# First gate tile loaded early and in two parts, first products by token block, softmax division on ScalarE

## Chip, cores and metric

The kernel runs on one core of a Trainium2 chip. The metric is device time in microseconds of one execution, with the median over the runs shown. Five engines matter: TensorE (PE), VectorE (DVE), ScalarE (ACT), GpSimd (POOL) and SyncE (SP, which only issues DMAs here). Each works through its own instructions in order.

## What is computed

One layer of a decoder over 512 tokens of width 1024, cut here to what the text speaks of:

```
xn = rms_norm(h, norm1_g)
u, v, q, c_kv, q_idx, k_idx, w_idx, gates = split(xn @ w_in)
y_a = chunked_spatial_gating(u, v, ...)
qh  = partial_rope(rms_norm(q), positions)
att = softmax(qh . k over the 128 keys that the indexer picked, causal)
y_b = att @ vv
merged = sigmoid(g_A) * (y_a @ w_a_out) + sigmoid(g_B) * (y_b @ w_b_out)
h  = h + merged @ w_o
hn = rms_norm(h, norm2_g)
h  = h + peer(hn)
```

`peer` scores 128 x 128 experts by product keys, takes 16 of them for each of 8 heads and token, and sums gate * gelu(hn . u_e) * v_e over them.

## The kernel before

Tokens are four blocks of 128. Products that need float32 accuracy go through `mm3`: both operands are split into a high and a low part, and three products are summed. A weight tile (128 x 1024) comes through `load_w`: SP loads `wraw`, ACT casts it to `whi`, DVE makes `wlo` as the difference. So each weight passes SP's queue, ACT and DVE in turn.

*Start.* The four x tiles are loaded (L195), transposed on PE eight times each (L203) into `ps_tr`, and split into `xh` (ACT, L205) and `xl` (DVE, L207). In between, `ck_weights` loads four weight tiles; when all is there, `tok_group` makes the first products, one PSUM tile per token block.

*Mixers.* Column tiles (`pcol`) are products of xh, xl with the columns of w_in, for u and for the gates `sg`. Query tiles `qs` are normalized, rotated on DVE (`rope`, L338 to L343) and transposed on PE (`pq`, L442). The top 128 keys are found on DVE by repeated MAX and MATCH_REPLACE (L465, L466); the spatial gating adds and multiplies `zt` (L493, L494). `attend(b)` (L499 to L528) makes the logits of four heads (`pa`, PE), adds the mask and takes the maximum (DVE, L507), makes the Exp (ACT, L510), the reciprocal (DVE, L511) and the division (DVE, L512), transposes the weights `at` on PE (`ptr`, L518), copies them out of PSUM (`pT`, L520: DVE and ACT in turn), and multiplies by the values (`py`, L524).

*Experts.* For the first three token blocks (384 tokens) all experts are computed densely, as 128 groups of 128: `expert_in(j)` loads up-row tile Uj, makes `pa` (24 products, 384 columns) and its Gelu; groups 28 to 99 keep the result `actd` in DRAM (`ad`). Meanwhile the gates are written to DRAM as `gd`, in 24 chunks of 16 tokens (L840, on ACT's queue). The fourth block's experts are gathered row by row by POOL and handled on DVE.

*Final stage* (L844 to L903). For each of 128 groups j: load down-row tile Vj; `pr` = act * gate on DVE (L886); split into `ph` (ACT, L890) and `pl` (DVE, L891); 18 products into six PSUM tiles `y`. The gates come as tiles `gg`, one for eight groups, from all 24 chunks of gd (L872). The remaining 28 up-row tiles are handled in this stage as well.

The order of instructions on each engine is not the program's: a scheduler rearranges them by its own simulation (`schedule_with_timeline_sim`), within the dependences and the buffers of the pools. So an edit at one place can move instructions elsewhere.

Of the kernel before, what the change touches and what calls it, by code (L numbers as in the profile page):

```python
# [9 lines left out]
F32 = mybir.dt.float32  # L10
# [4 lines left out]
AF = mybir.ActivationFunctionType  # L15
# [5 lines left out]
P = 128  # L21
S = 512
# [38 lines left out]
def kernel(ctx: ExitStack, tc: tile.TileContext, x, pos, cst, wtok, wsm, wcol, wkv, spt,  # L61
# [81 lines left out]
    with ExitStack() as c1:  # L143
# [10 lines left out]
        def tok_group(src, lhs_h, lhs_l, name, keep=None, done=None, finish=None):  # L154

            ps = [mm.tile([P, S], F32, name=f"{name}{b}", tag="mm") for b in range(NB)]

            def part(kp, b, hi, lo):
                bs = slice(b * P, (b + 1) * P)
                for kk in range(2):  # L160
                    k = 2 * kp + kk
                    ks = slice(kk * 512, (kk + 1) * 512)
                    mm3(ps[b], lhs_h[:, k, bs], lhs_l[:, k, bs], hi[:, ks], lo[:, ks], k == 0, k == KC - 1)

            if keep is None:
                for kp in range(4):
                    hi, lo = load_w(src(kp))
                    for b in range(NB):
                        part(kp, b, hi, lo)
            else:  # L170
                ws = keep if src is None else [load_w(src(kp), keep, 2) for kp in range(4)]
                for b in range(NB):
                    for kp in range(4):
                        part(kp, b, *ws[kp])
                    if done and 0 < b < NB - 1:
                        done(b - 1, ps[b - 1])
                if done:
                    finish(ps)
            return ps
# [3 lines left out]
        with tc.tile_pool(name="xin", bufs=4, reuse_waits="tile") as xp:  # L183
# [2 lines left out]
            ssx = tp.tile([P, NB], F32, name="ssx")  # L186
            ws = []

            def ck_weights(kp):
                ws.append(load_w(wtok[8 + kp], xp, 2))  # L190

            xts = []
            for b in range(NB):
                xt = xp.tile([P, D], F32, name="xt")
                SY.dma_start(xt, x[b * P:(b + 1) * P, :])  # L195
                xts.append(xt)
                if b == 0:
                    SY.dma_start(g1c, g1b)
                bs = slice(b * P, (b + 1) * P)
                for k0 in range(0, KC, 4):  # L200
                    ps = mm.tile([P, 4, P], F32, name="ps_tr", tag="mm")
                    for k in range(4):
                        T.transpose(ps[:, k, :], xt[:, (k0 + k) * P:(k0 + k + 1) * P], ident)  # L203
                    for k in range(k0, k0 + 4):
                        sq_after = A.activation(xh[:, k, bs], ps[:, k - k0, :], AF.Copy, scale=g1c[:, k:k + 1])  # L205
                    for k in range(k0, k0 + 4):
                        V.scalar_tensor_tensor(xl[:, k, bs], ps[:, k - k0, :], g1c[:, k:k + 1],  # L207
                                               xh[:, k, bs].bitcast(F32), ALU.mult, ALU.subtract)
                for _ in range((1, 0, 1, 2)[b]):
                    ck_weights(len(ws))  # L210
            ps_ck = tok_group(None, xh, xl, "pt2", ws)
            junk = xp.tile([P, D], F32, name="junk", bufs=1)
            with tc.issue_after(sq_after.ins):
                for b in range(NB):
# [284 lines left out]
        def attend(b):  # L499
            n = (b + 1) * P  # L500
            ph = []
            for h in range(NH):
# [9 lines left out]
                V.tensor_scalar(t, t, mx[:, 3:4], None, ALU.mult)  # L512
                ph.append(t)
            pts = []
            for k in range(b + 1):
                pt = sm.tile([P, S], F32, name="ptr", tag="sm")
                for h in range(NH):
                    T.transpose(pt[:, h * P:(h + 1) * P], ph[h][:, k * P:(k + 1) * P], ident)  # L518
                pT = sc.tile([P, S], F32, name="pT", tag="w", bufs=NW)
                (A.copy if k % 2 else V.tensor_copy)(pT, pt)  # L520
# [322 lines left out]

    with ExitStack() as c3:  # L844
        yp = c3.enter_context(tc.tile_pool(name="yp", bufs=1, space=PSUM))
        wv = c3.enter_context(tc.tile_pool(name="wv", bufs=2, reuse_waits="tile"))
        gr = c3.enter_context(tc.tile_pool(name="gr", bufs=2, reuse_waits="tile"))
# [16 lines left out]
        def load_v(n):  # L864
            while len(vq) < min(n, P):
                vq.append(load_w(vt[len(vq)], wv, 4))

        load_v(2)
        for j in range(P):
            if j % JG == 0:  # L870
                gt = gr.tile([P, NCH, JG, TC], F32, name="gg", tag="gg")
                SY.dma_start(gt, gd[:, :, j:j + JG, :])  # L872
                if j + JG == P:
                    hr = gr.tile([P, NB - 1, D], F32, name="hr", tag="gg")
# [99 lines left out]
```

## Time and profile before

| | |
|---|---|
| runs | 1598.69 us median of 3 (1598.64 to 1601.45) |
| profiled execution | 1599.28 us, span 1597.2 us |
| PE busy | 1558.5 us (98%) |
| DVE busy | 1271.2 us (80%) |
| ACT busy | 646.3 us (40%) |
| POOL busy | 346.0 us (22%) |
| mean DMA rate | 247 GB/s |

The span is from the first to the last instruction; the execution's time has some 2 us around it. PE is busy nearly throughout, so what matters is where it is not. The mean DMA rate hides a low first third and a final stage between 284 and 370 GB/s in most of its slices. Busy shares are means over stages, and a stage is read through its own windows and waits. Releasers in the list of waits are inferred; a busy PE can run at half its clock, which the column PEclk shows.

### The profile page before, as it was taken

The numbers are of one execution on the slowest core, as the hardware profiler recorded it, in microseconds if no ns is written. First come the engines' busy times: TensorE is split into PE (matmuls) and PEld (weight loads), VectorE is DVE, ScalarE is ACT, GpSimd is POOL, SyncE is SP. The second block draws the span as 40 slices with busy tenths as digits, with TensorE's granted clock in tenths as the row PEclk, the third lists the DMA queues.
The fourth block names the chain that finished last, engine by engine and source line by source line (L and its number), as shares of the span: only waits on it lengthen the run. The fifth ranks groups of instructions, "written<-read, shape, count | busy, mean of one in ns | idle before, by whom it ended". The sixth has DMA issues, their size and how long they took to land.

```text
span 1597.2 us, 22620 instructions
## 1 busy us (share of the span) xinstructions
PE 1558.5 (98%) x8173; PEld 1355.2 (85%) x8173; DVE 1271.2 (80%) x2670; ACT 646.3 (40%) x954; POOL 346.0 (22%) x280
## 2 busy tenths in 40 slices
PE   8999999999999999999999989999999999999998
PEld 6777867888899999999999978888888888888777
DVE  6489974557999989999999657787877877888854
ACT  5453333323334335555666533333333333333232
POOL 0010000000000353323222213433322332334400
PEclk9999999999999999999999989999999999999999
DMA  6111224222223689999999999999999999998862
GB/s 218 66 66 67 93 75 176 93 93 93 89 83 120 225 299 342 345 339 341 368 338 344 355 315 312 314 351 344 370 335 342 338 334 328 342 328 306 284 226 95
DMA packets 160400, 395.01 MB, mean 247 GB/s; under 512 B 12960, under 2 KB 80544, under 8 KB 156704
## 3 DMA queue, kind: packets, MB, share of 16 engines
q1 hardware_dynamic: 109600, 220.01, 39.5%
q0 software_dynamic: 36864, 134.23, 23.7%
q10 hardware_dynamic: 13824, 39.33, 6.3%
q8 instruction: 64, 1.05, 0.3%
q14 instruction: 48, 0.39, 0.1%
HBM read 350.53 MB, written 42.99 MB: 246 GB/s over the span
## 4 chain that ended last, share of the span: by engine, by line
PE 75%; DMA 12%; issue 5%; DVE 5%; POOL 2%; ACT 0%; SPq 0%; POOLq 0%; DVEq 0%; ACTq 0%
PE pa L93 8%; PE pa L91 8%; PE pa L92 8%; PE y L92 7%; PE y L93 7%; PE y L91 7%; DMA gt<-in_v_rows,eid 5%; DMA gt<-in_u_rows,eid 3%; PE pg L836 2%; PE pcol L91 2%; PE pcol L92 2%; PE pcol L93 2%; POOL gt L658 2%; PE pq L91 2%; PE pq L92 2%
## 5 line engine op out<-in xcount | busy, mean ns | idle before, releaser
L86 ACT CAST whi<-wraw 128x1024 fp32r<-128x1024 f32 x320 | 335.0, 1053 | 332.2 <-PE pa L92 124.2
L87 DVE TENSOR_TENSOR wlo<-wraw,whi 128x1024 fp32r<-128x1024 f32 x320 | 389.3, 1219 | 79.9 <-ACT whi L86 69.9
L91 PE MATMUL pa<-hh,whi 128*128 128x384 f32 (+2 forms) x1040 | 349.8, 336 | 2.9 <-ACT actd L649 2.2
L93 PE MATMUL pa<-hh,wlo 128*128 128x384 f32 (+2 forms) x1040 | 348.6, 336 | 2.7 <-DVE wlo L87 2.7
L92 PE MATMUL pa<-hl,whi 128*128 128x384 f32 (+2 forms) x1040 | 348.4, 335 | 0.0
L92 PE MATMUL y<-wlo,ph 128*128 128x512 f32 x768 | 302.5, 394 | 4.7 <-DVE wlo L87 4.7
L93 PE MATMUL y<-whi,pl 128*128 128x512 f32 x768 | 299.0, 392 | 0.0
L658 POOL DMA_INDIRECT gt<-in_u_rows,eid x128 | 168.9, 1319 | 535.7 <-DVE dots L664 306.8
L658 POOL DMA_INDIRECT gt<-in_v_rows,eid x128 | 164.7, 1287 | 293.2 <-DVE h2l L673 263.4
L890 ACT CAST ph<-pr 128x384 fp32r<-128x384 f32 x128 | 65.8, 515 | 384.4 <-PE y L92 360.4
L91 PE MATMUL y<-whi,ph 128*128 128x512 f32 x768 | 209.3, 393 | 7.7 <-ACT ph L890 7.7
L93 PEld LDWEIGHTS pa<-hh,wlo 128*128 128x128 f32 x1040 | 195.4, 188 | 8.2 <-DVE wlo L87 4.2
L91 PEld LDWEIGHTS pa<-hh,whi 128*128 128x128 f32 x1040 | 195.5, 188 | 7.9 <-ACT actd L649 2.9
L92 PEld LDWEIGHTS pa<-hl,whi 128*128 128x128 f32 x1040 | 195.5, 188 | 4.1
L673 DVE SCALAR_TENSOR_TENSOR h2l<-gt,coef,h2l 128x1024 f32<-128x1024 f32 x128 | 163.8, 1280 | 25.7 <-DMA gt<-in_v_rows,eid 25.3
L92 PEld LDWEIGHTS y<-wlo,ph 128*128 128x128 f32 x768 | 145.0, 189 | 35.6 <-DVE wlo L87 6.4
L91 PEld LDWEIGHTS y<-whi,ph 128*128 128x128 f32 x768 | 144.3, 189 | 34.8 <-ACT ph L890 8.0
L664 DVE CUSTOM_DVE_ANT_0 gt<-gt,hn 128x1024 f32<-128x1024 f32 x128 | 155.6, 1218 | 17.8 <-DMA gt<-in_u_rows,eid 17.7
L93 PEld LDWEIGHTS y<-whi,pl 128*128 128x128 f32 x768 | 144.6, 188 | 28.2
L891 DVE TENSOR_TENSOR pl<-pr,ph 128x384 fp32r<-128x384 f32 x128 | 71.1, 556 | 89.9 <-ACT ph L890 82.4
L838 ACT ACTIVATE ch<-pg 128x512 f32<-128x512 f32 x96 | 96.7, 1113 | 30.0 <-PE pg L836 29.6
L886 DVE TENSOR_TENSOR pr<-act,gg 128x384 f32<-128x384 f32 x128 | 70.5, 554 | 11.2 <-DMA act<-ad 4.9
(305 smaller groups left out, 1925.3 us busy)
## 6 DMA issues: line engine op xcount, KB each, us to landing
wraw<-in_ut SPq DMA_DIRECT2D x128, 512.0 KB, 5.9
wraw<-in_v_rows SPq DMA_DIRECT2D x128, 512.0 KB, 6.3
gd<-ch ACTq DMA_DIRECT2D x24, 1024.0 KB, 6.6
gg<-gd SPq DMA_DIRECT2D x16, 1536.0 KB, 14.4
ad<-actd ACTq DMA_DIRECT2D x72, 192.0 KB, 5.5
act<-ad SPq DMA_DIRECT2D x72, 192.0 KB, 6.8
wraw<-in_wcol SPq DMA_DIRECT2D x20, 512.0 KB, 3.2
wraw<-in_wq SPq DMA_DIRECT2D x16, 512.0 KB, 3.2
```

Of the source, the lines that this page charges most:

```text
L86: A.copy(hi, raw)
L87: V.tensor_tensor(lo, raw, hi.bitcast(F32), ALU.subtract)
L91: T.matmul(ps, lh, rh, start=start, stop=False)
L92: T.matmul(ps, lh, rl, start=False, stop=False)
L93: return T.matmul(ps, ll, rh, start=False, stop=stop)
L658: G.indirect_dma_start(out=t, out_offset=None, in_=table, in_offset=bass.IndirectOffsetOnAxis(ap=eid[:, s:s + 1], axis=0))
L664: V.tensor_tensor_reduce(out=t, in0=t, in1=hn3, scale=1.0, scalar=0.0, op0=ALU.mult, op1=ALU.add, accum_out=dots[:, s:s + 1])
L673: V.scalar_tensor_tensor(h2l, t, coef[:, s:s + 1], h2l, ALU.mult, ALU.add)
L838: A.activation(ch[:, :, to + t4:to + t4 + 4].rearrange("p i t -> p t i"), pg, AF.Copy, scale=1.0 / GS)
L886: V.tensor_tensor(pr.rearrange("p (c t) -> p c t", c=NCH), acts[j].rearrange("p (c t) -> p c t", c=NCH), gt[:, :, j % JG, :], ALU.mult)
L890: A.copy(ph, pr)
L891: V.tensor_tensor(pl, pr, ph.bitcast(F32), ALU.subtract)
```

## The change

Three edits:

- At the start, one weight tile is loaded behind each x tile, the first products are written by token block and weight (`PARTS`) between the transposes, and `ps_tr` takes its buffers from the pool of three instead of the pool of five.
- In `attend`, the division is an ACT instruction (Copy with a scale per row) and all pT copies are on ACT.
- In the final stage, the pool of `gg` is split into two of one buffer; the first is taken ahead of the pool of the V weights. `load_g(0)` is written ahead of the V loads and loads chunks 0 to 22 and chunk 23 by a DMA each; other groups are loaded as before.

```
@@ -168,7 +168,7 @@
                     for b in range(NB):
                         part(kp, b, hi, lo)
             else:
-                ws = keep if src is None else [load_w(src(kp), keep, 2) for kp in range(4)]
+                ws = [load_w(src(kp), keep, 2) for kp in range(4)]
                 for b in range(NB):
                     for kp in range(4):
                         part(kp, b, *ws[kp])
@@ -186,9 +186,19 @@
             ssx = tp.tile([P, NB], F32, name="ssx")
             ws = []
 
-            def ck_weights(kp):
-                ws.append(load_w(wtok[8 + kp], xp, 2))
-
+
+            ps_ck = [mm.tile([P, S], F32, name=f"pt2{b}", tag="mm") for b in range(NB)]
+
+            def ck_part(kp, b):
+                hi, lo = ws[kp]
+                bs = slice(b * P, (b + 1) * P)
+                for kk in range(2):
+                    k = 2 * kp + kk
+                    ks = slice(kk * 512, (kk + 1) * 512)
+                    mm3(ps_ck[b], xh[:, k, bs], xl[:, k, bs], hi[:, ks], lo[:, ks], k == 0, k == KC - 1)
+
+            PARTS = ((), ((0, 0), (0, 1)), ((1, 0), (1, 1), (0, 2), (1, 2)),
+                     ((2, 0), (2, 1), (2, 2), (0, 3), (1, 3), (2, 3), (3, 0), (3, 1), (3, 2), (3, 3)))
             xts = []
             for b in range(NB):
                 xt = xp.tile([P, D], F32, name="xt")
@@ -198,7 +208,7 @@
                     SY.dma_start(g1c, g1b)
                 bs = slice(b * P, (b + 1) * P)
                 for k0 in range(0, KC, 4):
-                    ps = mm.tile([P, 4, P], F32, name="ps_tr", tag="mm")
+                    ps = sm.tile([P, 4, P], F32, name="ps_tr", tag="sm")
                     for k in range(4):
                         T.transpose(ps[:, k, :], xt[:, (k0 + k) * P:(k0 + k + 1) * P], ident)
                     for k in range(k0, k0 + 4):
@@ -206,9 +216,9 @@
                     for k in range(k0, k0 + 4):
                         V.scalar_tensor_tensor(xl[:, k, bs], ps[:, k - k0, :], g1c[:, k:k + 1],
                                                xh[:, k, bs].bitcast(F32), ALU.mult, ALU.subtract)
-                for _ in range((1, 0, 1, 2)[b]):
-                    ck_weights(len(ws))
-            ps_ck = tok_group(None, xh, xl, "pt2", ws)
+                ws.append(load_w(wtok[8 + b], xp, 2))
+                for kp, bb in PARTS[b]:
+                    ck_part(kp, bb)
             junk = xp.tile([P, D], F32, name="junk", bufs=1)
             with tc.issue_after(sq_after.ins):
                 for b in range(NB):
@@ -509,7 +519,7 @@
                 V.tensor_scalar(mx[:, 1:2], mx[:, 0:1], -ATT_SCALE, None, ALU.mult)
                 A.activation(t, t, AF.Exp, bias=mx[:, 1:2], scale=ATT_SCALE, accum_out=mx[:, 2:3])
                 V.reciprocal(mx[:, 3:4], mx[:, 2:3])
-                V.tensor_scalar(t, t, mx[:, 3:4], None, ALU.mult)
+                A.activation(t, t, AF.Copy, scale=mx[:, 3:4])
                 ph.append(t)
             pts = []
             for k in range(b + 1):
@@ -517,7 +527,7 @@
                 for h in range(NH):
                     T.transpose(pt[:, h * P:(h + 1) * P], ph[h][:, k * P:(k + 1) * P], ident)
                 pT = sc.tile([P, S], F32, name="pT", tag="w", bufs=NW)
-                (A.copy if k % 2 else V.tensor_copy)(pT, pt)
+                A.copy(pT, pt)
                 pts.append(pT)
             py = sm.tile([P, S], F32, name="py", tag="sm")
             for k in range(b + 1):
@@ -843,8 +853,9 @@
 
     with ExitStack() as c3:
         yp = c3.enter_context(tc.tile_pool(name="yp", bufs=1, space=PSUM))
+        gr = [c3.enter_context(tc.tile_pool(name="gr0", bufs=1, reuse_waits="tile"))]
         wv = c3.enter_context(tc.tile_pool(name="wv", bufs=2, reuse_waits="tile"))
-        gr = c3.enter_context(tc.tile_pool(name="gr", bufs=2, reuse_waits="tile"))
+        gr.append(c3.enter_context(tc.tile_pool(name="gr1", bufs=1, reuse_waits="tile")))
         cp = c3.enter_context(tc.tile_pool(name="cp", bufs=3, reuse_waits="tile"))
         ys = [[yp.tile([P, 512], F32, name=f"y{b}_{hf}") for hf in range(2)] for b in range(NB - 1)]
         vt = v_rows.rearrange("(i j) d -> i j d", j=P)
@@ -865,13 +876,20 @@
             while len(vq) < min(n, P):
                 vq.append(load_w(vt[len(vq)], wv, 4))
 
+        def load_g(i):
+
+            t = gr[i % 2].tile([P, NCH, JG, TC], F32, name="gg", tag="gg")
+            for c0, c1 in ((0, NCH - 1), (NCH - 1, NCH)) if i == 0 else ((0, NCH),):
+                SY.dma_start(t[:, c0:c1], gd[:, c0:c1, i * JG:(i + 1) * JG, :])
+            return t
+
+        gt0 = load_g(0)
         load_v(2)
         for j in range(P):
             if j % JG == 0:
-                gt = gr.tile([P, NCH, JG, TC], F32, name="gg", tag="gg")
-                SY.dma_start(gt, gd[:, :, j:j + JG, :])
+                gt = load_g(j // JG) if j else gt0
                 if j + JG == P:
-                    hr = gr.tile([P, NB - 1, D], F32, name="hr", tag="gg")
+                    hr = gr[P // JG % 2].tile([P, NB - 1, D], F32, name="hr", tag="gg")
                     SY.dma_start(hr, hd)
             room = max(KEPT - 5 - max(0, KEPT - j), 0) + max(0, j - AHEAD)
             while len(acts) < min(P, AHEAD + min(room, (P - AHEAD) * (j + 1) // (P - 4))):
```

The scheduler gives another order with it. Three places:

SP, the end of the up-row loads and the start of the down-row loads (in_ut are up-rows, in_v_rows down-rows; x98 stands for U2 to U99). Before, then with the change:

```order
43 L85 DMA wraw<-in_ut 128x1024 x98
44 L85 DMA wraw<-in_v_rows 128x1024 x2
45 L872 DMA gg<-gd 128x24x128
46 L85 DMA wraw<-in_v_rows 128x1024 x2
47 L872 DMA gg<-gd 128x24x128
48 L85 DMA wraw<-in_ut 128x1024 x2
```

```order
43 L85 DMA wraw<-in_ut 128x1024 x95
44 L883 DMA gg<-gd 128x23x128
45 L85 DMA wraw<-in_ut 128x1024 x3
46 L883 DMA gg<-gd 128x128
47 L85 DMA wraw<-in_v_rows 128x1024 x4
48 L883 DMA gg<-gd 128x24x128
49 L85 DMA wraw<-in_ut 128x1024 x2
```

The first gg is now two loads, one issued three up-row loads earlier and one directly ahead of V0; the second gg follows V3 as before.

PE, the fourth query block's attention: pa are logits, ptr the transposes of the softmax rows, pcol a column tile. Before, then with the change; shown are the rows at which the kind of work changes, and the row numbers tell what lies between.

```order
821 L504 MATMUL pa<-kT,qs_951 128x512 x2
822 L92 MATMUL pcol_2237<-xl,whi 128x512
829 L93 MATMUL pcol_2237<-xh,wlo 128x512
830 L504 MATMUL pa<-kT,qs_951 128x512 x2
831 L518 MATMUL ptr<-ident,at 128x128 x16
832 L524 MATMUL py<-pT,vv 128x512 x4
```

```order
818 L514 MATMUL pa<-kT,qs_951 128x512
819 L93 MATMUL pcol_2237<-xh,wlo 128x512
823 L91 MATMUL pcol_2237<-xh,whi 128x512
824 L528 MATMUL ptr<-ident,at 128x128
825 L92 MATMUL pcol_2237<-xl,whi 128x512
831 L528 MATMUL ptr<-ident,at 128x128
832 L92 MATMUL pcol_2237<-xl,whi 128x512
835 L92 MATMUL pcol_2237<-xl,whi 128x512
836 L528 MATMUL ptr<-ident,at 128x128 x2
837 L93 MATMUL pcol_2237<-xh,wlo 128x512
840 L93 MATMUL pcol_2237<-xh,wlo 128x512
841 L528 MATMUL ptr<-ident,at 128x128 x12
```

Before, all 16 transposes follow the last logits at once; now pcol products stand between them, 19 from the last logits to the last twelve transposes.

DVE, the end of the query rotation (qs_948 to qs_951 are the four blocks; sg a gate product). Before, then with the change, the rows of the halves that write qs and what stands between:

```order
269 L466 MATCH_REPLACE madd_646<-m_1303,madd_646 128x384
270 L342 TENSOR_TENSOR qs_948<-rp_990,rp_991 128x4x16
271 L343 TENSOR_TENSOR qs_948<-rp_992,rp_993 128x4x16
272 L342 TENSOR_TENSOR qs_949<-rp_1010,rp_1011 128x4x16
273 L343 TENSOR_TENSOR qs_949<-rp_1012,rp_1013 128x4x16
274 L536 TENSOR_TENSOR sg_1854<-pcol_1829,rxb 128x512
284 L87 TENSOR_TENSOR wlo<-wraw,whi 128x1024
286 L342 TENSOR_TENSOR qs_950<-rp_1030,rp_1031 128x4x16
287 L343 TENSOR_TENSOR qs_950<-rp_1032,rp_1033 128x4x16
289 L343 TENSOR_TENSOR qs_951<-rp_1052,rp_1053 128x4x16
```

```order
275 L476 MATCH_REPLACE madd_646<-m_1303,madd_646 128x384
276 L546 TENSOR_TENSOR sg_1854<-pcol_1829,rxb 128x512
277 L352 TENSOR_TENSOR qs_948<-rp_990,rp_991 128x4x16
278 L353 TENSOR_TENSOR qs_948<-rp_992,rp_993 128x4x16
279 L87 TENSOR_TENSOR wlo<-wraw,whi 128x1024
280 L352 TENSOR_TENSOR qs_949<-rp_1010,rp_1011 128x4x16
281 L353 TENSOR_TENSOR qs_949<-rp_1012,rp_1013 128x4x16
291 L476 MATCH_REPLACE madd_646<-m_1306,madd_646 128x384
292 L352 TENSOR_TENSOR qs_950<-rp_1030,rp_1031 128x4x16
293 L353 TENSOR_TENSOR qs_950<-rp_1032,rp_1033 128x4x16
295 L353 TENSOR_TENSOR qs_951<-rp_1052,rp_1053 128x4x16
```

The gate product now stands ahead of the first block's rotation and a wlo between the first and the second; the wlo ahead of the third is gone from there.

## Rows read from the trace of the kernel before

**Rows 1.** The page's part 1, whole span: busy us of each engine (share) xinstructions

```profile
PE 1558.5 (98%) x8173; PEld 1355.2 (85%) x8173; DVE 1271.2 (80%) x2670; ACT 646.3 (40%) x954; POOL 346.0 (22%) x280
```

**Rows 2.** Waits of PE, whole span: us in total, times, longest us

```profile
PE y L91 <- ACT ph L890: 7.7, 1, 7.7
...
PE ps_tr L203 <- DMA xt<-in_x: 7.7, 3, 4.2
...
PE y L92 <- DVE wlo L87: 4.7, 4, 1.5
...
PE pq L442 <- DVE qs L343: 3.3, 1, 3.3
...
PE ptr L518 <- DVE at L512: 2.5, 2, 2.4
```

**Rows 3.** PE's timeline at four places: start us, us, ..., [idle before <-releaser]

```profile
230.54 0.39 PE L91 MATMUL pcol<-xh,whi 128*128 128x512 f32 x1
230.77 0.39 PE L92 MATMUL pcol<-xl,whi 128*128 128x512 f32 x1
...
237.80 0.44 PE L518 MATMUL ptr<-ident,at 128*128 128x128 f32 x2 [2.38 <-DVE at L512]
...
909.59 0.44 PE L91 MATMUL pa<-hh,whi 128*128 128x384 f32 x1 [1.35 <-ACT actd L649]
...
925.90 0.79 PE L91 MATMUL y<-whi,ph 128*128 128x512 f32 x1 [7.72 <-ACT ph L890]
```

**Rows 4.** 3-us windows, 909 to 933: width, busy us (instructions), PEclk, DMA share, GB/s

```profile
909.00:912.00 3.00, 2.41 (x14) 2.41 (x15) 2.82 (x4) 1.03 (x3) 0.18 (x1) 1.00 0.84 253
...
924.00:927.00 3.00, 1.10 (x3) 0.91 (x4) 2.15 (x5) 0.98 (x2) 0.00 (x0) 0.50 1.07 358
927.00:930.00 3.00, 3.00 (x9) 2.32 (x8) 1.96 (x4) 0.51 (x1) 0.00 (x0) 0.50 1.21 291
930.00:933.00 3.00, 3.00 (x11) 2.39 (x10) 0.00 (x0) 0.51 (x1) 0.00 (x0) 0.70 1.11 358
```

**Rows 5.** SP's timeline, 897 to 909: start us of each load's issue

```profile
897.96 0.33 SPq L85 DMA_DIRECT2D wraw<-in_ut  x1
...
906.70 1.56 SPq L85 DMA_DIRECT2D wraw<-in_v_rows  x2
908.35 0.61 SPq L872 DMA_DIRECT2D gg<-gd  x1
```

**Rows 6.** ACT's timeline, 890 to 930: its last gd store and U97's cast

```profile
893.76 0.33 ACTq L840 DMA_DIRECT2D gd<-ch  x1
...
908.10 1.04 ACT L86 CAST whi<-wraw 128x1024 fp32r<-128x1024 f32 x1 [3.11 <-PE pa L92]
```

**Rows 7.** DMA of 890 to 930: a queue's packets, MB, share; issues with median us to landing

```profile
q1 hardware_dynamic: 6860, 7.56, 61.0%
...
wraw<-in_ut SPq DMA_DIRECT2D x6, 512.0 KB, 6.2
...
wraw<-in_v_rows SPq DMA_DIRECT2D x6, 512.0 KB, 7.4
...
gd<-ch ACTq DMA_DIRECT2D x1, 1024.0 KB, 8.4
```

**Rows 8.** A 4-us window in the fourth query block, columns as in rows 4

```profile
240.00:244.00 4.00, 4.00 (x11) 2.01 (x10) 0.16 (x1) 0.59 (x1) 0.00 (x0) 0.71 0.99 383
```

**Rows 9.** The page's part 6, whole span: KB each, us to landing

```profile
wraw<-in_v_rows SPq DMA_DIRECT2D x128, 512.0 KB, 6.3
```

**Rows 10.** Groups by line, whole span: xcount | busy us, mean ns | idle before

```profile
L510 ACT ACTIVATE at<-at,mx 128x128 f32<-128x128 f32 (+3 forms) x16 | 8.9, 556 | 14.4 <-DVE mx L509 14.3
...
L512 DVE TENSOR_SCALAR at<-at,mx 128x128 f32<-128x128 f32 (+3 forms) x16 | 5.9, 377 | 0.1
```

**Rows 11.** DVE's timeline in the fourth query block

```profile
234.83 1.22 DVE L87 TENSOR_TENSOR wlo<-wraw,whi 128x1024 fp32r<-128x1024 f32 x1
```

**Rows 12.** A 50-us window of the final stage, columns as in rows 4

```profile
1075.00:1125.00 50.00, 49.21 (x233) 42.40 (x232) 40.17 (x46) 17.61 (x24) 20.53 (x15) 1.00 0.99 353
```

More of the change, by code (lines that the diff above doesn't have):

```diff
@@ L170, in tok_group @@
             else:
-                ws = keep if src is None else [load_w(src(kp), keep, 2) for kp in range(4)]
+                ws = [load_w(src(kp), keep, 2) for kp in range(4)]
                 for b in range(NB):
@@ L187, with ck_part @@
             ws = []
-            def ck_weights(kp):
-                ws.append(load_w(wtok[8 + kp], xp, 2))
+            ps_ck = [mm.tile([P, S], F32, name=f"pt2{b}", tag="mm") for b in range(NB)]
+            def ck_part(kp, b):
+                hi, lo = ws[kp]
+                bs = slice(b * P, (b + 1) * P)
+                for kk in range(2):
+                    k = 2 * kp + kk
+                    ks = slice(kk * 512, (kk + 1) * 512)
+                    mm3(ps_ck[b], xh[:, k, bs], xl[:, k, bs], hi[:, ks], lo[:, ks], k == 0, k == KC - 1)
+            PARTS = ((), ((0, 0), (0, 1)), ((1, 0), (1, 1), (0, 2), (1, 2)),
+                     ((2, 0), (2, 1), (2, 2), (0, 3), (1, 3), (2, 3), (3, 0), (3, 1), (3, 2), (3, 3)))
             xts = []
@@ L200 @@
                 for k0 in range(0, KC, 4):
-                    ps = mm.tile([P, 4, P], F32, name="ps_tr", tag="mm")
+                    ps = sm.tile([P, 4, P], F32, name="ps_tr", tag="sm")
                     for k in range(4):
@@ L208 @@
                                                xh[:, k, bs].bitcast(F32), ALU.mult, ALU.subtract)
-                for _ in range((1, 0, 1, 2)[b]):
-                    ck_weights(len(ws))
-            ps_ck = tok_group(None, xh, xl, "pt2", ws)
+                ws.append(load_w(wtok[8 + b], xp, 2))
+                for kp, bb in PARTS[b]:
+                    ck_part(kp, bb)
             junk = xp.tile([P, D], F32, name="junk", bufs=1)
@@ L511, in attend @@
                 V.reciprocal(mx[:, 3:4], mx[:, 2:3])
-                V.tensor_scalar(t, t, mx[:, 3:4], None, ALU.mult)
+                A.activation(t, t, AF.Copy, scale=mx[:, 3:4])
                 ph.append(t)
@@ L519, in attend @@
                 pT = sc.tile([P, S], F32, name="pT", tag="w", bufs=NW)
-                (A.copy if k % 2 else V.tensor_copy)(pT, pt)
+                A.copy(pT, pt)
                 pts.append(pT)
@@ L845 @@
         yp = c3.enter_context(tc.tile_pool(name="yp", bufs=1, space=PSUM))
+        gr = [c3.enter_context(tc.tile_pool(name="gr0", bufs=1, reuse_waits="tile"))]
         wv = c3.enter_context(tc.tile_pool(name="wv", bufs=2, reuse_waits="tile"))
-        gr = c3.enter_context(tc.tile_pool(name="gr", bufs=2, reuse_waits="tile"))
+        gr.append(c3.enter_context(tc.tile_pool(name="gr1", bufs=1, reuse_waits="tile")))
         cp = c3.enter_context(tc.tile_pool(name="cp", bufs=3, reuse_waits="tile"))
@@ L866, in load_v, with load_g @@
                 vq.append(load_w(vt[len(vq)], wv, 4))
+        def load_g(i):
+            t = gr[i % 2].tile([P, NCH, JG, TC], F32, name="gg", tag="gg")
+            for c0, c1 in ((0, NCH - 1), (NCH - 1, NCH)) if i == 0 else ((0, NCH),):
+                SY.dma_start(t[:, c0:c1], gd[:, c0:c1, i * JG:(i + 1) * JG, :])
+            return t
+        gt0 = load_g(0)
         load_v(2)
@@ L870 @@
             if j % JG == 0:
-                gt = gr.tile([P, NCH, JG, TC], F32, name="gg", tag="gg")
-                SY.dma_start(gt, gd[:, :, j:j + JG, :])
+                gt = load_g(j // JG) if j else gt0
                 if j + JG == P:
-                    hr = gr.tile([P, NB - 1, D], F32, name="hr", tag="gg")
+                    hr = gr[P // JG % 2].tile([P, NB - 1, D], F32, name="hr", tag="gg")
                     SY.dma_start(hr, hd)
```

## The prediction

> **What bounds the kernel now.** I read the busy shares first, then what TensorE (PE) waits for, then the rows around its longest wait. PE is busy for 1558.5 of 1597.2 us [rows 1], so 38.7 us are all the idle time there is. The list of its waits names most of it [rows 2]: 7.7 us before the first product into y in the final stage, 7.7 us for x tiles at the start, 4.7 us for wlo in the final stage, 3.3 us for the rotated queries qs, 2.5 us for softmax rows `at`. The reader should see that only a few waits are there to be removed, and that a wait can cost more than itself: PE ends its last product before y at 918.18 and starts again at 925.90 [rows 3]; afterwards the granted clock stands at 0.50 (1.2 of 2.4 GHz) and comes back within 930 to 933 [rows 4].
>
> **Part 1, the first group's gates.** What PE waits for at 918.18 is ph, which ACT makes from pr, which multiplies by the tile gg. The load of gg was issued at 908.35 [rows 5], behind those of V0 and V1 (both from 906.70). Its source was complete before that: the last store of gd was issued at 893.76 [rows 6], and such a store takes 8.4 us [rows 7], so 902.2. The load was late because it stood late in SyncE's (SP's) order.
>
> The change issues 23 of its 24 chunks behind the weight load of U96, three loads before the old place of V0 (first piece of order above), and the last chunk, which alone needs the last store, behind U99. Both parts land well before PE needs them. What goes is 7.72 us of idle and the time lost at half clock behind it, which is PE's busy time multiplied by the missing clock in three windows [rows 4]: 1.10 x 0.50 + 3.00 x 0.50 + 3.00 x 0.30 = 2.95 us. Ceiling: 10.7 us.
>
> What takes its place: the DMA engines are full there (share 1.07 to 1.21 [rows 4]), so 1.5 MB put ahead of other loads delays them. Behind part 1 in SP's queue stand U97, U98, U99, the last chunk, V0 and V1. How long part 1 (23/24 of 1.57 MB, 1.51 MB) holds them up is bounded by two rates: all that the engines move, 336 GB/s (the mean of 358, 291 and 358 [rows 4]), gives 4.5 us; what SP's queue had of it, 7.56 MB in 40 us [rows 7], 189 GB/s, gives 8.0 us.
> - U97 was issued at 897.96 [rows 5] and such a load lands 6.2 us later [rows 7], near 904.2. Its cast on ACT began at 908.10, when PE let go of a buffer [rows 6]: slack 3.9 us. Late by 4.5 to 8.0, the cast starts 0.6 to 4.1 us later. ACT works in order; behind the cast stands the Gelu `actd` that frees a PSUM buffer of PE. PE already waits 1.35 us for it [rows 3], and that wait grows by 0.6 to 4.1 us.
> - V0 was issued at 906.70, so it was there after 7.4 us [rows 7], at 914.1; now at 918.6 to 922.1. With its cast (1.04 us, as in [rows 6]) y can start at 919.6 to 923.2. PE itself gets there at 918.8 to 922.3, so V0 is late next, by some 0.8 us.
>
> So y starts 2.7 to 6.3 us before 925.90, and with 2.95 us of clock part 1 brings 5.7 to 9.2. I take -7.5, the middle: the two rates are equally near.
>
> One rule bears on the grown wait. The rows show that the clock stayed at 1.00 around the wait of 1.35 us [rows 3, 4] and stood at a mean of 0.71 behind the wait of 2.38 us at 237.80 [rows 3, 8]. The Trainium skill, "TensorE: Matmul & The Clock Gate", Part 1, says that the throttled clock is the default and that activity releases it. By that rule a wait at 909 that has grown to 2.0 to 5.5 us may halve the clock too, and the gain would then be smaller by about the 1.2 us that the slow stretch at 240 cost (worked out below). I don't put it into the sum, since the products that it would slow have some 0.8 us until V0 comes; it widens the range.
>
> Against this part speaks a second rule. On full engines [rows 4] a load of a down-row took 7.4 us to land [rows 7], where the median of all 128 is 6.3 [rows 9]. The Trainium skill, "DMA: Bandwidth & Descriptors", in Queues, rings and completion order, says that each engine consumes the descriptors of one row in ring order. By it a load put in front pays for itself with the loads behind; that is the rival of the moved wait, below.
>
> **Part 2, the softmax.** 16 divisions leave VectorE (DVE), 5.9 us in all, 0.377 each [rows 10]. On ACT each costs about what the Exp of the same tiles does, 0.556 us [rows 10], together 8.9 us, on an engine that is busy 40% of the span [rows 1]. Neither sum is the term; PE's wait is. In the fourth query block a wlo of 1.22 us at 234.83 [rows 11] stands on DVE between the maxima and the last two Exps, PE has only transposes left in its order, and waits 2.38 us for the divisions [rows 3]. The change moves PE's order as well (second piece of order): between the last logits and the last twelve transposes now stand 19 column products that take 0.23 us each [rows 3], 4.4 us of cover. The wait of 2.5 us should go, and with it the slow stretch, 4.00 x 0.29 = 1.16 us in 240 to 244 [rows 8]: ceiling 3.7. I take -3.2, for the last two Exps and divisions still follow each other on ACT.
>
> The order changes at 138 to 152 too, where PE waits 3.3 us for qs [rows 2] (third piece). A gate product sg now stands before the first query's rotation and a wlo between the first and the second; the wlo that stood before the third is no longer there. Three more pairs of MAX and MATCH_REPLACE come before zt, which PE also needs. Bounds: -0.5 (the wlo gone from the third) to +2.3 us (sg and the pairs all on the path). I take +0.9, the middle. Part 2: -2.3, bounds -4.2 to +2.3.
>
> **Part 3, the start.** Of the three waits for x, 7.7 us [rows 2], two stay, since x0, the first weights and x1 are loaded in the same order. The third, 0.38 us, goes, for a product can run while x2 comes. Transposes have three buffers for five; no order there makes one wait on it. -0.3; bounds -0.4 to +1.0.
>
> **The final stage.** PE starts it some 5 us earlier while the DMA engines run at a share up to 0.99 [rows 12], so weights have less lead. PE waited 4.7 us in four places for wlo [rows 2]. I add one: a wlo takes 1.22 us [rows 11]. +1.2, bounds 0 to +5.
>
> **The sum:** -7.5 - 2.3 - 0.3 + 1.2 = -8.9 against the profiled execution's 1599.28, 1590.4. The median of the runs shown, 1598.69, is 0.6 lower, and against it the sum gives 1589.8. I say 1590.
>
> **The rivals.**
> - *A larger gain.* U97 meets a queue that part 1 has left already, the wait at 909 doesn't grow, and y starts at 918.2: -10.7, and -3.7 for the softmax, 1583 to 1586. For it: the engines had room at 909 to 912 (0.84 [rows 4]). Against: they are over 1.0 soon after. Chance 0.17.
> - *The wait moves.* Part 1 delays U97 by 8 us, PE waits 5.5 us at 909, the clock halves there, and the final stage returns more through wlo. What is left is 1 to 5 us: 1594 to 1598. For it: the full engines [rows 4]. Against: the slack of 3.9 us. Chance 0.15, about half of it on either side of the bound below.
> - *Slower.* The DMA engines pace the final stage: an earlier start takes the lead away, and PE meets a wlo not yet made, 1.22 us at a time. Eight such waits eat the gain of 9 to 10; from eleven on the kernel is slower, 12 to 14 of them give 1603 to 1606. For it: share 0.99, and four such waits today. Against: in that same window PE is busy 49.21 of 50 us [rows 12]. Chance 0.06.
> - *Part 1 does nothing.* The last chunk waits behind three loads that themselves wait for buffers, and lands as late as gg did. Only the softmax is left: 1596 to 1598. Against: V0 stood behind the same three loads and was issued at 906.70, before gg [rows 5]. Chance 0.07.
>
> **How the numbers follow.** The forecast, 1587 to 1594, has 0.55. A measurement of this kernel tells about 0.2%, 3.2 us, from no change. Faster by more: 0.55 + 0.17 + 0.08 = 0.80; within: 0.07 + 0.07 = 0.14; slower: 0.06. The range 1583 to 1597 holds the forecast, the larger gain and most of the moved wait.
>
> **What would show it.** Right: no wait of y for ph beyond 2 us; clock 1.00 from 921 to 933; the wait for `actd` at 909 grown to 2 to 5 us; waits of ptr under 1 us; the qs wait at 3 to 5; waits for wlo in y of 4 to 7 us. Wrong: a wait of y for ph over 3 us, one of over 6 us before it, or over 10 us for wlo in y.

## The result and the profile after

The changed kernel takes 1593.43 us (median of 15 runs) against 1600.97 us for the kernel before in the same runs: ratio 0.9949, 95% interval 0.9929 to 0.9969, some 8 us. The two profiled executions differ by less: spans of 1597.2 and 1591.7 us, 5.5 us. Single runs of either kernel lie up to about 0.5% from their median, 8 us, so the verdicts are read from the ratios. The parts are read from the traces, one for each kernel, and a part of two or three us in one trace can be chance.

PE's waits in the changed kernel (us in total, times, longest), to be held against [rows 2]:

```profile
PE pa L91 <- ACT actd L659: 10.0, 4, 6.8
PE ps_tr L213 <- DMA xt<-in_x: 6.8, 2, 4.2
PE y L92 <- DVE wlo L87: 4.5, 2, 3.7
PE pq L452 <- DVE qs L353: 3.6, 3, 1.7
...
PE ptr L528 <- ACT pT L530: 0.5, 1, 0.5
...
PE y L91 <- ACT ph L908: 0.2, 1, 0.2
```

The wait of y for ph is gone, 7.7 us, and the waits for softmax rows are gone. But the wait for `actd`, one of 1.35 us before [rows 3], is now 6.8 us long at one place. PE's timeline places it: the first product behind the last attention block, the wait, and the first product into y.

```profile
239.84 0.74 PE L91 MATMUL pwo<-yh,whi 128*128 128x512 f32 x2 [0.68 <-ACT yh L537]
...
909.41 0.69 PE L91 MATMUL pa<-hh,whi 128*128 128x384 f32 x1 [6.79 <-ACT actd L659]
...
920.23 1.08 PE L91 MATMUL y<-whi,ph 128*128 128x512 f32 x4
```

Before, the same product pwo started at 245.69:

```profile
245.69 0.73 PE L91 MATMUL pwo<-yh,whi 128*128 128x512 f32 x2 [0.68 <-ACT yh L527]
```

So 5.85 us were won by the end of attention. The first product into y comes at 920.23 where it came at 925.90 [rows 3], 5.67 earlier: up to there the gates' early load added nothing. Between the two places lies one more loss, at 648.56, where a wait of 2.37 us was followed by 3.4 us at a clock of 0.53:

```profile
648.56 0.69 PE L91 MATMUL pa<-hh,whi 128*128 128x384 f32 x1 [2.37 <-ACT actd L659]
```

```profile
648.60:652.00 3.40, 3.29 (x20) 2.82 (x21) 3.40 (x5) 3.40 (x4) 1.20 (x1) 0.53 0.91 324
```

PE's waits between 540 and 700 sum to 5.2 us before and 4.5 now, but this clock costs 3.29 x 0.47 = 1.6 us. What the early load did to the clock is seen in 3-us windows (columns as in [rows 4]):

```profile
906.00:909.00 3.00, 0.00 (x0) 0.00 (x0) 0.00 (x1) 1.08 (x2) 0.00 (x0) 0.80 1.02 405
909.00:912.00 3.00, 2.59 (x8) 2.59 (x9) 3.00 (x4) 0.85 (x2) 0.36 (x1) 0.50 1.04 405
912.00:915.00 3.00, 3.00 (x12) 3.00 (x11) 2.57 (x6) 0.51 (x1) 2.62 (x2) 0.56 1.03 402
...
921.00:924.00 3.00, 3.00 (x15) 2.47 (x14) 2.68 (x3) 0.31 (x1) 0.00 (x0) 1.00 1.18 314
924.00:927.00 3.00, 3.00 (x15) 2.49 (x14) 2.05 (x3) 1.85 (x3) 0.00 (x0) 1.00 1.02 383
```

The half clock, which stood behind y's first product, now stands behind the wait for `actd`: 2.59 x 0.50 + 3.00 x 0.44 = 2.6 us lost where 2.95 were. Idle and clock together cost 1.35 + 7.72 + 2.95 = 12.0 us around this place before and 6.79 + 2.6 = 9.4 us now. By these two traces part 1 brought 2.6 us.

More than that was lost again late in the final stage. A single wait for wlo there, 3.7 us, was followed by a slower clock. The first two rows are DVE's: it stands for a gathered row tile of the fourth block, and the wlo that PE waits for comes behind it.

```profile
1492.70 1.28 DVE L683 SCALAR_TENSOR_TENSOR h2l<-gt,coef,h2l 128x1024 f32<-128x1024 f32 x1 [3.29 <-DMA gt<-in_v_rows,eid]
...
1494.37 1.22 DVE L87 TENSOR_TENSOR wlo<-wraw,whi 128x1024 fp32r<-128x1024 f32 x1
```

```profile
1495.65 0.80 PE L92 MATMUL y<-wlo,ph 128*128 128x512 f32 x1 [3.71 <-DVE wlo L87]
```

```profile
1490.00:1525.00 35.00, 31.29 (x132) 26.06 (x131) 26.29 (x30) 8.39 (x13) 8.29 (x8) 0.90 0.79 280
```

31.29 x 0.10 = 3.1 us of clock. The kernel before waited 4.7 us for wlo in four pieces, the longest 1.5 [rows 2], and the same window had a clock of 1.00.

### The profile page after: what moved, and what is told of

Same layout as the page of the kernel before. It is cut to its first block, busy times and chain, and to the rows that moved or that the text cites. A ratio compares the mean times of both kernels' runs of the same rounds, so it can differ in the third digit from the quotient of the medians.

```text
span 1591.7 us, 22605 instructions
## 1 busy us (share of the span) xinstructions
PE 1559.4 (98%) x8173; PEld 1359.1 (85%) x8173; DVE 1265.2 (79%) x2648; ACT 657.5 (41%) x976; POOL 345.4 (22%) x280
## 4 chain that ended last, share of the span: by engine, by line
PE 78%; DMA 9%; issue 6%; DVE 3%; POOL 2%; ACT 1%; SPq 0%; POOLq 0%; DVEq 0%; ACTq 0%
PE pa L93 9%; PE pa L91 9%; PE pa L92 9%; PE y L92 7%; PE y L93 7%; PE y L91 7%; DMA gt<-in_v_rows,eid 5%; PE pg L846 3%; POOL gt L668 2%; PE pcol L92 2%; PE pcol L91 2%; PE pcol L93 2%; PE pq L91 2%; PE pq L92 2%; PE pq L93 2%
## 5 line engine op out<-in xcount | busy, mean ns | idle before, releaser
L668 POOL DMA_INDIRECT gt<-in_u_rows,eid x128 | 177.9, 1390 | 527.9 <-DVE dots L674 308.8
L668 POOL DMA_INDIRECT gt<-in_v_rows,eid x128 | 155.3, 1213 | 308.8 <-DVE h2l L683 276.3
L91 PEld LDWEIGHTS y<-whi,ph 128*128 128x128 f32 x768 | 143.7, 188 | 26.9 <-ACT ph L908 0.5
```

The lines of the kernel that those rows point to most:

```text
L668: G.indirect_dma_start(out=t, out_offset=None, in_=table, in_offset=bass.IndirectOffsetOnAxis(ap=eid[:, s:s + 1], axis=0))
```

## The experiments

**Which part brings it.** Two kernels carry one half of the change each.

e1 against the changed kernel (the gates' load put back; here and below, ... stands for lines left out):

```diff
...
-        gt0 = load_g(0)
         load_v(2)
         for j in range(P):
             if j % JG == 0:
-                gt = load_g(j // JG) if j else gt0
+                gt = gr.tile([P, NCH, JG, TC], F32, name="gg", tag="gg")
+                SY.dma_start(gt, gd[:, :, j:j + JG, :])
...
```

e2 against the changed kernel (the start and the softmax put back):

```diff
...
-                ws.append(load_w(wtok[8 + b], xp, 2))
-                for kp, bb in PARTS[b]:
-                    ck_part(kp, bb)
+                for _ in range((1, 0, 1, 2)[b]):
+                    ck_weights(len(ws))
+            ps_ck = tok_group(None, xh, xl, "pt2", ws)
...
-                A.activation(t, t, AF.Copy, scale=mx[:, 3:4])
+                V.tensor_scalar(t, t, mx[:, 3:4], None, ALU.mult)
...
-                A.copy(pT, pt)
+                (A.copy if k % 2 else V.tensor_copy)(pT, pt)
```

> The start and the softmax as changed, the gates' load as before. Theory 1 (the softmax brought the whole gain and the early gates' load only moved PE's wait from y to pa): ratio 0.9955 to 0.9975, and in the profile the last block of attention ends 5 to 6 us earlier than before, y waits 7 to 9 us for ph, no wait for actd over 2 us. Rival (the gates' load brought half or more, the softmax 2 to 3 us): ratio 0.998 to 0.999.

> Only the gates' load is changed; start and softmax as before. Theory 1: ratio 0.998 to 1.001; the wait for actd at the end of the up-row loads is 6 to 8 us, the wait for ph is gone, and the first product into y starts within 1 us of 925.9. Rival: ratio 0.9945 to 0.997 and the first product into y 4 us or more earlier than 925.9.

e1 has ratio 0.9988 (0.9966 to 1.0009), e2 0.9971 (0.9951 to 0.9990). First e1's rows, then e2's, from PE's timeline:

```profile
239.96 0.73 PE L91 MATMUL pwo<-yh,whi 128*128 128x512 f32 x2 [0.68 <-ACT yh L537]
...
916.59 0.80 PE L91 MATMUL y<-whi,ph 128*128 128x512 f32 x1 [7.63 <-ACT ph L900]
```

```profile
916.09 0.69 PE L91 MATMUL pa<-hh,whi 128*128 128x384 f32 x1 [7.52 <-ACT actd L649]
```

Each half does in its place what it does in the whole: e1 ends attention 5.7 us early and keeps the wait for ph, e2 loses the wait for ph and has 7.5 us for `actd` instead, with the first product into y at 926.16, 0.3 us later than before. But both ratios miss what was expected: e1's lies outside 0.9955 to 0.9975 and in the range of its rival, e2's outside 0.998 to 1.001 and beside the range of its rival. In e1 PE reaches y 9.3 us earlier than before, 3.6 earlier than the changed kernel, since it has no wait over 0.6 us between 540 and 700 and no slow clock there. Its span ends only 1.5 us earlier than before; its waits for wlo in y grew from 4.7 to 10.0 us:

```profile
PE y L92 <- DVE wlo L87: 10.0, 5, 4.2
```

So a gain ahead of the final stage can be returned there. By ratios alone the halves can't be told apart: the intervals overlap. The profiles give the larger part to start and softmax, the ratios to the gates; how the 8 us divide is not shown.

**Why PE waits for `actd`.** Part 1 moved behind U99, the up-row loads ahead of it.

```diff
...
-        SY.dma_start(raw, src)
+        raw_dma.append(SY.dma_start(raw, src))
...
-        gt0 = load_g(0)
+        with tc.issue_after(raw_dma[-1].ins):
+            gt0 = load_g(0)
```

> As the changed kernel, but part 1 of the gates' load is issued behind U99 instead of behind U96, ahead of V0. If part 1's place ahead of U97 makes PE wait for actd, that wait falls from 6.8 us to under 2 us, and V0 is late instead: part 1 holds the queue for 8 to 13 us, so y starts at 916 to 921 and the ratio is 0.993 to 0.997. Rival (the actd wait has another cause, such as the ad stores): the wait stays at 5 us or more.

The ratio is 0.9987 (0.9962 to 1.0011), not the expected 0.993 to 0.997. The wait for `actd` is back at 1.35 us, as the reading of a queue held up says, and V0 is late by more than expected, with y at 922.01 instead of 916 to 921:

```profile
922.01 1.22 PE L93 MATMUL y<-whi,ph 128*128 128x512 f32 x2 [10.78 <-ACT whi L88]
```

In the changed kernel, e2 and e3 the load makes PE wait 7 to 11 us where its 1.5 MB stand ahead of a weight that PE needs soon. How long it holds the queue is read from single issues in the changed kernel (median us to landing of the one load issued): U96 at 887.10, part 1 at 887.70, U97 at 892.34.

```profile
wraw<-in_ut SPq DMA_DIRECT2D x1, 512.0 KB, 6.5
```

```profile
gg<-gd SPq DMA_DIRECT2D x1, 1472.0 KB, 18.5
```

```profile
wraw<-in_ut SPq DMA_DIRECT2D x1, 512.0 KB, 15.5
```

U96 landed at 893.6 and part 1 at 906.2: 12.6 us in which no other load of SP's landed, 1.51 MB / 12.6 = 120 GB/s. U97 took 15.5 us and its cast started at 907.92 on landing. SP itself stood still:

```profile
892.34 9.58 SPq L85 DMA_DIRECT2D wraw<-in_ut  x3
```

Three issues that take 0.33 us each when nothing stands before them ([rows 5] has one) took 9.58, 8.63 of it U97's own. The kernel before shows the same at V2, behind its load of gg at 908.35 [rows 5]:

```profile
909.01 11.93 SPq L85 DMA_DIRECT2D wraw<-in_v_rows  x1
```

**Is it the size of the pieces?** gd laid out by groups, so that part 1 is one run of 11.5 KB per partition instead of 23 runs of 512 bytes; the stores of gd get the small pieces instead.

```diff
-    gd = dram.tile([P, NCH, P, TC], F32, name="gd")
+    gd = dram.tile([P, P // JG, NCH, JG, TC], F32, name="gd")
...
-                A.dma_start(gd[:, b * (P // TC) + cc], ch)
+                A.dma_start(gd[:, :, b * (P // TC) + cc], ch.rearrange("p (g j) t -> p g j t", j=JG))
...
-                SY.dma_start(t[:, c0:c1], gd[:, c0:c1, i * JG:(i + 1) * JG, :])
+                SY.dma_start(t[:, c0:c1], gd[:, i, c0:c1])
```

> The changed kernel with the gates stored in DRAM by groups of eight, so that the load of a group reads one run of 12 KB per partition (11.5 KB for part 1) instead of 24 runs of 512 bytes; the stores write runs of 512 bytes instead. If the small pieces make part 1 hold SP's queue for 12.6 us (U96 landed at 893.6, part 1 at 906.2), it now holds it 4 to 6 us, U97 lands at 898 to 901, the actd wait falls from 6.8 to under 2.5 us; the ratio is 0.990 to 0.994. Rival (the time is the engines' bandwidth alone, shared by bytes): part 1 holds the queue for 10 us or more and the wait stays above 5 us; or the stores, now in small pieces, delay the up-rows by as much.

The load issued ahead of it at 902.15 landed after 6.3 us, at 908.4; part 1, issued at 903.48, after 10.4, at 913.9. It held the queue for 5.4 us instead of 12.6, within the expected 4 to 6, and the wait for `actd` at the end of the up-rows is 2.2 us. This pair alone doesn't show that the pieces did it, for ACT's queue moved 1.35 MB during the 12.6 us and 0.09 MB during the 5.4. The loads of all groups do: the kernel before, then e7, with the median time to landing.

```profile
gg<-gd SPq DMA_DIRECT2D x16, 1536.0 KB, 14.4
```

```profile
gg<-gd SPq DMA_DIRECT2D x15, 1536.0 KB, 9.8
```

The ratio is 0.9994 (0.9971 to 1.0017) all the same, not 0.990 to 0.994. As the rival had it, the stores pay: those of gd land after 10.2 us in the median (6.3 in the changed kernel), and `actd` waits sum to 15.7 us. The longest, 6.0 at 749.73, ends with a Gelu that had stood until a store of `actd` landed; before it, one issue on ACT's queue took 4.12 us, and the Gelu behind it stood for that:

```profile
735.22 4.12 ACTq L660 DMA_DIRECT2D ad<-actd  x1
739.45 0.49 ACT L659 ACTIVATE actd<-pa 128x384 f32<-128x384 f32 x1 [4.26 <-issue]
...
749.18 0.49 ACT L659 ACTIVATE actd<-pa 128x384 f32<-128x384 f32 x1 [7.36 <-DMA ad<-actd]
```

**Smaller steps.** The 24 chunks of the first group in six loads, each soon after its chunks are stored.

```diff
-            for c0, c1 in ((0, NCH - 1), (NCH - 1, NCH)) if i == 0 else ((0, NCH),):
+            for c0, c1 in ((0, 6), (6, 12), (12, 18), (18, 21), (21, NCH - 1), (NCH - 1, NCH)) if i == 0 else ((0, NCH),):
```

> As the changed kernel, but the first group's gates are loaded in six pieces of 6, 6, 6, 3, 2 and 1 chunks, each issued soon after its last chunk is stored. Theory 1 with the queue as its cause: each piece holds the queue for 1 to 3 us, the weights' slack of 3 to 4 us covers it, no wait for actd over 1.5 us at the end, none of y for ph; the first product into y starts at 911 to 914 and the ratio is 0.990 to 0.993. Rival (the DMA engines are full from 650 us on, so any piece put ahead delays the up-rows just as much): waits for actd or wlo of 5 us or more in sum between 650 and 905, ratio 0.994 to 0.997.

Ratio 0.9962 (0.9939 to 0.9986), in the rival's range and not in the expected 0.990 to 0.993. The long wait for `actd` is gone (the longest is 1.76 us), but y waits 6.98 us for ph again, at 904.55 in an order in which y starts before the last up-rows. This time not for gates: DVE, which makes pr, stands for 4.86 us until a gathered row tile of the fourth block's experts has landed.

```profile
902.25 1.22 DVE L674 CUSTOM_DVE_ANT_0 gt<-gt,hn 128x1024 f32<-128x1024 f32 x1 [4.86 <-DMA gt<-in_u_rows,eid]
903.40 0.08 DVE L674 DVE_READ_ACCUMULATOR2_ANT dots<- 128x1 f32 x1
903.40 1.02 DVE L904 TENSOR_TENSOR pr<-act,gg 128x384 f32<-128x384 f32 x2
```

**What returns the gain in the final stage.** The same kind of wait was suspected behind wlo, as the rows at 1492.70 show it for one. A fourth buffer for gathered tiles, with one expert group fewer kept on the chip to make room, in the kernel before (e5), the changed one (e6) and the one with six pieces (e8).

```diff
-    KEPT = 28
+    KEPT = 27
...
-    gat = ctx.enter_context(tc.tile_pool(name="gat", bufs=3, reuse_waits="tile"))
+    gat = ctx.enter_context(tc.tile_pool(name="gat", bufs=4, reuse_waits="tile"))
```

> The kernel before with four buffers for gathered rows instead of three (KEPT 27 instead of 28 makes room: one expert group more goes through DRAM). Theory 2: in the final stage the gathers of the fourth block set the pace from about 1465 to 1525 us, since DVE waits in order for a gathered tile and wlo stands behind it. A fourth buffer issues each gather one tile earlier: DVE's waits for gt, 43 us before, fall under 25 us, PE's waits for wlo in y from 4.7 to under 2 us, ratio 0.995 to 0.999. Rival (the lead of the weights ends because the DMA engines are full): waits for wlo in y stay at 4 us or more, ratio 0.999 to 1.003.

> The changed kernel with the same fourth gather buffer. Theory 2: what the mixers won (5.9 us in the profile) now reaches the end whole, so that against the run with four buffers and without the change the span is 7 to 10 us shorter, and the ratio to the kernel before is 0.989 to 0.993; the actd wait at the end of the up-rows stays at 5 to 8 us. Rival (no absorption by the gathers): the difference to the run with four buffers and without the change is the same 5 to 6 us as the two profiles show with three.

> The six pieces with the fourth gather buffer. Theory 2: in the run with six pieces the first product into y waited 7.0 us for ph because DVE stood 4.9 us on a gathered tile ahead of pr; with four buffers that wait is under 3 us, the wlo waits in y are under 2 us, and the ratio is 0.987 to 0.991, below all kernels so far. Rival: ratio 0.993 or more, with a wait of y for ph over 5 us.

DVE's waits for gathered tiles, first in the kernel before, then in e5:

```profile
DVE h2l L673 <- DMA gt<-in_v_rows,eid: 25.3, 21, 2.6
DVE gt L664 <- DMA gt<-in_u_rows,eid: 17.7, 18, 2.3
```

```profile
DVE gt L664 <- DMA gt<-in_u_rows,eid: 5.3, 8, 2.3
DVE h2l L673 <- DMA gt<-in_v_rows,eid: 0.6, 2, 0.3
```

43.0 us fell to 5.9, and the list of PE's waits in e5 has none for wlo in y, where there were 4.7 us. With the rows at 1492.70 this says that the gathers held wlo back. It is not a clean test, since e5 also has three groups of up-rows more behind the first product into y (272 products of each kind into `pa` against 248), whose time gives the weights more lead. The times went the other way and missed all three expected ratios: 1.010 (1.007 to 1.013) for e5, 1.003 (1.0011 to 1.005) for e6, 0.9986 (0.9968 to 1.0004) for e8. In e5 PE waits 14.8 us in 17 places for `actd` during the up-rows and 11.1 us for ph; in e8, where the wait for ph is gone as expected, 15.8 us in 14 places for `actd`. Whether the fourth buffer or the smaller KEPT makes these kernels slower was not tested. Between e5 and e6, the same two edits apart, the change is worth 1614.7 - 1604.9 = 9.8 us of span, and the ratios give 1.003 / 1.010 = 0.993; with three buffers the spans differ by 5.5. e6 keeps a wait of 8.9 us for `actd`, so the four microseconds more may be what the final stage does not return; two single traces don't show it.

**What in the softmax brings it.** The division alone (e9), and with the pT copies (e10).

e9 is the kernel before with the first of these edits, e10 with both:

```diff
-                V.tensor_scalar(t, t, mx[:, 3:4], None, ALU.mult)
+                A.activation(t, t, AF.Copy, scale=mx[:, 3:4])
...
-                (A.copy if k % 2 else V.tensor_copy)(pT, pt)
+                A.copy(pT, pt)
```

> Only the division moved to ACT; pT copies on DVE and ACT in turn, start and gates as before. PE's order in the fourth query block is as in the kernel before: all 16 transposes directly behind the last logits. If the gain of the mixers comes from the products that now stand between logits and transposes, nothing is won here: PE waits 2 to 5 us for at, and the last block of attention ends (first product into pwo behind it) at 244.5 to 248, before 245.7. Rival (DVE without the divisions is what helps): 240 to 243.

> Division and pT copies on ACT; start and gates as before. In PE's order column products stand between the last logits and the last 15 transposes. If these products are the cover, the first product into pwo behind the last block comes at 239.5 to 242 (before 245.7, changed kernel 239.8), PE's wait for at is under 1 us and the clock stays at 1.0 from 236 to 248. Since the final stage returns part of it, ratio 0.996 to 1.000. Rival (the start's edit is needed for it, through the order that it sets): 243 or later.

The first products into pwo before and behind the four blocks of attention, e9 and then e10:

```profile
148.61 0.71 PE L91 MATMUL pwo<-yh,whi 128*128 128x512 f32 x2
...
243.71 0.73 PE L91 MATMUL pwo<-yh,whi 128*128 128x512 f32 x2 [0.68 <-ACT yh L527]
```

```profile
150.85 0.70 PE L91 MATMUL pwo<-yh,whi 128*128 128x512 f32 x2
...
241.16 0.73 PE L91 MATMUL pwo<-yh,whi 128*128 128x512 f32 x2 [0.68 <-ACT yh L527]
```

The stretch between them, in the kernel before and in the changed one (columns as in [rows 4]):

```profile
150.62:245.69 95.07, 91.03 (x380) 67.53 (x379) 75.47 (x191) 35.32 (x66) 0.00 (x0) 0.98 0.26 94
```

```profile
149.93:239.84 89.91, 88.73 (x380) 66.72 (x379) 66.74 (x165) 45.75 (x88) 0.00 (x0) 1.00 0.22 77
```

It lasts 95.1 us before (150.62 to 245.69) and with the division alone, 90.3 with the copies, 89.9 in the changed kernel (149.93 to 239.84). e9's end, 243.71, lies 2.0 us before the old 245.69, but its stretch starts 2.0 us earlier too; e9 ran once, in 1603.75 us. The stretch hardly scatters: it is 94.6 to 95.4 us in the four traces with the copies as before and 89.9 to 90.3 in the ten with all copies on ACT. In e9 PE's order has all 16 transposes of the fourth block directly behind the last logits, as before; in e10 13 column products stand between the last logits and the last 15 transposes. So the division on ACT was worth nothing by itself here; with the copies on ACT and the order that comes with them the stretch is 5 us shorter. Copies and order were not tested apart. For the order speaks that PE waits 1.67, 1.21 and 0.57 us between its transposes in e9 and 0.90 us once in e10, where the 13 products stand. e10 has ratio 0.9958 (0.9931 to 0.9985), about the whole result without start and gates, but e1, with the same softmax, has 0.9988.

**A faster version.** The fourth block's work in the final stage kept from being ordered more than 16 groups ahead on DVE, in the changed kernel (e11) and with the six pieces (e12).

```diff
...
-            V.tensor_tensor(pl, pr, ph.bitcast(F32), ALU.subtract)
+            pls.append(V.tensor_tensor(pl, pr, ph.bitcast(F32), ALU.subtract))
...
-            feed()
+            with tc.issue_after(pls[j - 16].ins) if j >= 16 else nullcontext():
+                feed()
```

> The changed kernel, with the handling of gathered rows in the final stage kept from being ordered more than 16 groups ahead on DVE: the order ends the gathers at group 121 instead of 116. If gathered tiles that have not landed are what holds wlo back, DVE's waits for gt fall from 43 to 25 to 38 us and PE's waits for wlo in y from 4.5 to under 3 us; ratio 0.992 to 0.995. Rival (the rate of three buffers is the limit, whatever the order): both sums as before within 1.5 us, ratio 0.994 to 0.997.

> The six pieces with the same limit on DVE's order. If both readings hold, the wait of 6.8 us for actd stays gone and the waits for wlo in y fall from 5.4 (six pieces alone) to under 3 us: ratio 0.990 to 0.994, the lowest of all. Rival: the first product into y still waits 5 us or more for ph behind a gathered tile, and the ratio is 0.994 to 0.998.

The ratios are as expected, 0.9924 (0.9897 to 0.9952) and 0.9907 (0.9873 to 0.9940), the lowest of all; the reason is another. The waits for wlo in y rose to 12.5 and 10.5 us instead of falling, and DVE's for gathered tiles from 43.0 to 60.6 and 55.9. What fell is the loss where the up-rows end. The 40 us from 900 on, in the kernel before, the changed one and e12:

```profile
900.00:940.00 40.00, 30.93 (x146) 27.60 (x145) 22.99 (x32) 13.60 (x19) 5.73 (x6) 0.87 1.04 356
```

```profile
900.00:940.00 40.00, 33.22 (x162) 30.75 (x161) 25.18 (x36) 13.50 (x19) 8.44 (x6) 0.91 1.03 365
```

```profile
900.00:940.00 40.00, 38.99 (x204) 35.95 (x203) 25.19 (x37) 14.49 (x21) 9.87 (x7) 1.00 0.92 327
```

PE's busy time times its clock is 26.9, 30.2 and 39.0 of 40 us. In e12 y starts at 895.9 and the last up-rows follow between the products into y, so a late weight of one kind can be covered by products of the other; e4's wait of 6.98 us for ph is gone, and PE's longest wait from 900 to 940 is 1.01 us. e12's span is 1587.2 us, 4.5 below the changed kernel, and it takes 1587.91 us in the median. Its interval still overlaps that of the changed kernel, and e11's single profile is no shorter (1592.7): that e12 beats the kernel before is shown, that it beats the changed one is likely only.

## Why the prediction was right

The forecast was 1590 us and 0.54% below the median of before; measured are 1593.4 and 0.51% (ratio 0.9949). The time lies in the range, its terms were not met, and that they sum to nearly the right total is luck: part 1 brought 4.9 us less than its term, parts 2 and 3 brought 3.25 more. By the spans of the two profiles the gain is 5.5 us, not 8.9. Of the signs named ahead, the clock from 921 to 933 and the waits for ph, ptr, qs and wlo came as those of being right; the wait for `actd`, 6.8 us, passed the 2 to 5 expected and is the one of over 6 us before y that was named as a sign of being wrong.

- **Part 1, -7.5.** Half right: the load was late only by its place, it vanished as y's wait, and the half clock behind it with it. Wrong is the step that bounds how long part 1 holds SP's queue, 4.5 to 8.0 us: it held it for 12.6. Hence U97's cast started when the load landed, 15.5 us after its issue, and the wait for `actd` grew by 5.4 us instead of 0.6 to 4.1. The second bound took the queue's mean rate over 40 us, 189 GB/s, in which weights of large pieces are mixed; the load alone got 120. A row of the kernel before would have warned: its sixteen loads of gg took 14.4 us to land in the median, where those of V took 6.3 [rows 9]. The term measured -2.6. The rival of the moved wait describes this place well, down to the clock that halves there; its time, 1594 to 1598, was missed by 0.6 us in the median, since part 2 was larger.
- **The rule on the clock.** The wait of 6.79 us halved the clock as the one of 2.38 had, at 2.6 us. The Trainium skill, "TensorE: Matmul & The Clock Gate", Part 1, has the throttled clock as the default that activity lifts. The trace agrees: the clock is 0.50 behind this wait and 1.00 from 915 on. The sum had left this loss out.
- **Part 2, -2.3.** Undersized. The cover by column products came as described, and the waits for softmax rows and the slow stretch at 240 went; the stretch of four blocks shrank by 5.2 us, not 3.2. In the stretch PE is idle for 4.0 us before and 1.2 now, 2.9 less, and busy 2.3 less with as many products, of which some 1.4 are clock (1.16 in 240 to 244 and 1.49 x 0.14 = 0.2 in 236 to 240); 0.9 stays open. The reshuffled query rotation cost no 0.9: PE waits 3.6 us in three pieces for 3.3 in one, and reached pwo at 149.93, 0.7 before its old time. The prediction priced the division and took the new order as given; e9 and e10 show that the order comes with the copies.
- **Part 3, -0.3.** Idle time for x fell from 7.7 to 6.8 us, and the third wait went: right, and small. The five traces with the old start have 7.3 to 7.7 us, the nine with the new one 6.5 to 7.5.
- **The final stage, +1.2.** Mis-sized: 4.7 us of waits for wlo stayed 4.5, but one of 3.7 cost 3.1 us of clock. The reason given, DMA engines running full, misses what stood ahead of that wlo: the rows at 1492.70 have a gathered tile on DVE, and in e5 these waits and those for wlo went together.

In profiles the terms read -5.85 (parts 2 and 3), -2.6 (part 1) and +2.9 (final stage: 3.1 of clock, 0.2 less of waits). Between 540 and 700 come -0.7 of waits and +1.6 of clock at 648.56, which no term had. They sum to -4.7 where the spans differ by 5.5. Whether the runs' 8 us instead of 5.5 are chance in two single traces stays open.

## What to carry to other kernels

A load that PE doesn't need for 20 us can still cost PE its wait, if a weight that is needed in 5 us stands behind it in the same queue: price it by how long loads of the same piece size took in that queue, not by the mean rate. Look for cover as other work of the late engine, in its order, rather than for shorter chains; in the attention here and in the best version of all, products of another kind stand where PE had waited. And before adding up gains ahead of a stage, ask what in that stage runs at its own pace.

## What was not expected of the hardware

- With other queues active, a load of 1.51 MB in runs of 512 bytes held SP's queue for 12.6 us (120 GB/s), the same bytes in runs of 11.5 KB for 5.4 us (279 GB/s); ACT's queue moved 1.35 MB during the first and 0.09 MB during the second. Over all groups such loads landed after 14.4 and 9.8 us in the median.
- An engine that issues into a held queue stands still itself: 8.63 us for one issue on SP, and 4.12 us for one on ACT, which had Gelus to compute.
- One wait of 3.71 us cost another 3.1 us in clock and one of 2.37 us another 1.6, while four waits of 0.8 to 1.5 us, 4.7 in all, cost none.
